# Hybrid FoX/RWKV-7 block on one core: odd chunks in the other PSUM half, q and k stored once per pair, some work reordered or moved between engines

## The chip, the core and the metric

The kernel runs on one core of a Trainium2 chip. That core has a matrix engine (TensorE, PE in the tables; its weight loads are listed apart as PEld), three other compute engines (VectorE = DVE, ScalarE = ACT, GpSimd = POOL), and SyncE (SP), which issues most DMA transfers. Each engine works through its own queue in order. Data live in device memory, in SBUF (128 partitions) and in PSUM, where matmul results land. The metric is the device time in microseconds (us) of one execution; smaller is better.

## The reference

One transformer block on a sequence of 1024 tokens, width 1024, all in float32. Two token mixers run side by side on the same normalised input `u`, and a convolutional feed-forward network follows.

```python
proj = u @ w_in                        # q,k,v,f | r,k,v,lora inputs | two gates
# FoX attention, 8 heads of 64: causal softmax with a forget term
logits = q @ k.T * 64 ** -0.5 + cum[:, None] - cum[None, :]     # cum = cumsum(log_sigmoid(f + b))
o_fox = softmax(causal(logits)) @ v
# RWKV-7, 8 heads of 64: a state of 64 x 64 per head, one step per token
def step(state, r_t, w_t, k_t, v_t, a_t, b_t):
    sa = state @ a_t
    state = state * w_t + outer(sa, b_t) + outer(v_t, k_t)
    return state, state @ r_t
y = groupnorm(y) * ln_w + ln_b
o_rwkv = (y + sum(r * k * r_k) * v) * g                         # the second term is the bonus
merged = sigmoid(gate_fox) * (o_fox @ fox_w_out) + sigmoid(gate_rwkv) * (o_rwkv @ rwkv_w_out)
h = h + gate1 * (merged @ w_o)
h = h + gate2 * conv_ffn(modulate(rms_norm(h)))
```

## The kernel before, in words

**Stages.** Read off the trace, in us from the start of the span: to 85 the modulation and the norm; to 200 the low-rank products and the first projections; to 600 the RWKV recurrence; to 622 its tail and the first late gates; to 838 the FoX attention; to 1050 the output projections; to 1647 the feed-forward network. Large products are three products of a value split in a high and a low part (`u_hi`, `u_lo`, `hi_in`, `lo_in`).

**The recurrence.** The 1024 tokens are cut into chunks of 64. A unit is one pair of heads `p` (4) and one half `hf` of the sequence (2): 8 units of 8 chunks (`NCU`) and two heads. `pre` (L698) prepares a unit: `cum`, the running sum of decays (two scans, L715), its exponentials `el` (L719) and `en` (L721), scaled keys `bk` (L739 and L744, with a copy into the other rows on ACT at L740), the chunk products `E`, and a blockwise inversion by 31 forward-substitution steps on DVE (`t` at L784, `E` at L786) from a matrix `M` that comes back by DMA. It also fills `QA` (L811, L823) and `bon`, the bonus (L827), from the product `bs` of `head_sums` (L690). `main` (L830) then forms `uw` (L863 to L872): per chunk and head a 64x64 weight `TT` times a 64x128 operand `QA`, 16 products of two records each. Head 0 lies in partitions 0 to 63, head 1 in 64 to 127, and each head's product goes to the same half of a PSUM tile; four chunks share a tile. DVE copies one half of the columns to `Wt` (L870), ACT the other to `UV` (L872). `mz` (L875 to L885) does the same with `Wt` as weight and `E` as operand; DVE adds its results into `Zt` (L882) and `Mt` (L884). Then a chain over the chunks follows: a product `sp` on PE, and the next state `S` on ACT (L903).

**What sets the order.** PE's order is written by the program. `Weave` runs generators (`pre_chain`, `main_chain`) on a clock of its own estimates and fills the gaps with steps of large products (`ps_rkv`, `qk`, `v`, `gt`). DVE, ACT, GpSimd and SP get their order in the recurrence from a scheduler that sorts by readiness and by `add_manual_dep`, which places an instruction behind another without a wait. In the attention DVE's and ACT's order follows the program too.

**Projections that pass through memory.** `qk_steps` (L386) makes q and k; ACT evacuates the high part `qh` (L393), DVE the low part `ql` (L395), and SP stores each to `d_st`, some twice, so that one transfer loads a head. `gate_steps` (L327 to L342) makes the merge gates: Abs, Exp, Ln, a combination on DVE, Exp, and a store to `d_gate`; the last of these run when the attention has begun.

**Attention.** `load_head` (L993) lets GpSimd issue three loads per head (`stA`, `stB`, `vh`). Three chains follow: logits `lg` and softmax (`nm` L1049 row maximum, `P` L1053 exponential, L1059 normalising), transposes `tp` with a split `th`, `tl` (L1086, L1089), and products `ov` with v. `collect` (L1114) runs 32 times, 4 per head: ACT copies one half of `ov`'s rows to `o` (L1120), DVE adds the other half (L1122); after four of them GpSimd makes the split `fx` (L1129, L1130). All products go through `mm` (L141). Late products `rk_ps` fill PE's gaps.

Of the kernel before, what the change touches and what calls it, by code (L numbers as in the profile page):

```python
# [9 lines left out]
F32 = mybir.dt.float32  # L10
# [122 lines left out]
def hybrid_block(ctx: ExitStack, tc: tile.TileContext, a, out):  # L133
# [13 lines left out]
    def f32(ap):  # L147
        return ap.bitcast(F32)
# [35 lines left out]
    nw0 = cp.tile([128, 4], F32, name="nw0")  # L184
    nc.vector.tensor_scalar(nw0, V("w0", 0, 4), -1.0, None, op0=ALU.mult)
    na0 = cp.tile([128, 4], F32, name="na0")
    nc.vector.tensor_scalar(na0, V("a0", 0, 4), -1.0, None, op0=ALU.mult)
    nkk = cp.tile([128, 4], F32, name="nkk")
    nc.vector.tensor_scalar(nkk, V("k_k", 0, 4), -1.0, None, op0=ALU.mult)
    oka = cp.tile([128, 4], F32, name="oka")  # L190
# [13 lines left out]
    d_st = dr.tile([8, 4, 128, S], F32R, name="d_st")  # L204
# [39 lines left out]
    marks = {}  # L244
    late_lo = deque()
# [81 lines left out]
    def gate_steps(w, i, pps, ptag, pool, tag):  # L327
# [3 lines left out]
        for hf in range(2):  # L331
# [4 lines left out]
            g = pool.tile([128, NH], F32, tag=tag, name=f"gs{i}_{hf}")  # L336
            nc.scalar.activation(g, ps, AF.Abs)
# [3 lines left out]
            nc.scalar.activation(g, g, AF.Exp)  # L341
# [4 lines left out]
    with ExitStack() as es:  # L346
# [39 lines left out]
        def qk_steps(w, i):  # L386
            sc_ = 0.125 if i < 4 else 1.0
            for hf in range(2):
# [169 lines left out]
        with tc.tile_pool(name="lg", bufs=1, reuse_waits="tile") as lg, \  # L558
# [65 lines left out]
            def forget():  # L624
# [10 lines left out]
                for hf in range(2):  # L635
# [28 lines left out]
                    nc.sync.dma_start(f32(d_st[:, 2, 64:68, cs]), f32(r[:, 0:4, :]))  # L664
                    nc.sync.dma_start(f32(d_st[:, 3, 64:68, cs]), f32(r[:, 2:6, :]))
# [24 lines left out]
        def head_sums(ps, x, hi, lo):  # L690

            nc.scalar.copy(hi, x)
            nc.gpsimd.tensor_tensor(lo, x, f32(hi), op=ALU.subtract)
            yield 3400
            mm(ps, blk_r, hi, start=True, stop=False)
            mm(ps, blk_r, lo, start=False, stop=True)

        def pre(k, p, hf):  # L698
# [41 lines left out]
            nc.scalar.copy(bk[64:128, :, 2, :], bk[64:128, :, 0, :])  # L740
# [40 lines left out]
            for s in range(31):  # L781
                J, W = s // 4 + 1, 31 - s
                tv = t32[:, 0 : J * W].rearrange("p (j w) -> p j w", w=W)
                tt(tv, E32[:, 0:J, s : s + 1].to_broadcast([128, J, W]),  # L784
                   M32[:, s : s + 1, s + 1 : 32].to_broadcast([128, J, W]), op=ALU.mult)
# [41 lines left out]
            tt(bon, bp, vv, op=ALU.mult)  # L827
            units[p, hf] = dict(ready=ready, pcd=pcd, ar=ar, E=E, QA=QA, TT=TT, bon=bon, UV=UV)

        def main(k, p, hf):  # L830
# [32 lines left out]
            for c0 in range(0, NCU, 4):  # L863
                ps = gen(f"uw{n}{c0}")
                for c in range(c0, c0 + 4):
                    for h in range(2):
                        x = (c - c0) * 128
                        mm(ps[HS[h], x : x + 128], TT[HS[h], c, :], QA[HS[h], c, :, :], start=True, stop=True)
                pv = ps.rearrange("p (c a s) -> p c a s", a=2, s=CH)
                nc.vector.tensor_copy(Wt[:, c0 : c0 + 4, :], pv[:, :, 1, :])  # L870
                for h in range(2):
                    nc.scalar.copy(UV[HS[h], c0 : c0 + 4, h, :], pv[HS[h], :, 0, :])  # L872
# [1165 lines left out]
```

## Time and profile before

| what | us |
|---|---|
| median of three runs | 1649.11 |
| lowest and highest | 1647.68, 1651.02 |
| the profiled execution's own time | 1648.91 |
| span of its trace | 1647.1 |

The profiled execution lies 0.2 us under the median, and 1.8 us of its time lie outside the span. The mean clock that was granted to PE was 0.995 of full speed. Rows of the profile read as: start, duration, engine, line, operation, output tile, inputs, the rows by the columns of the weight, the shape of the result, and how many records the row stands for; "[2.31 <-DVE ql L395]" behind a row says how long the engine had stood before it and what ended that.

### The profile page before, as it was taken

To read this page: it belongs to the slowest core of one execution; us is meant where nothing else is said; L and a number is where in the kernel's file an instruction comes from. 1 tells how busy PE (TensorE), PEld (TensorE's weight loads), DVE (VectorE), ACT (ScalarE), POOL (GpSimd) and SP (SyncE) were. 2 spreads that over 40 slices of the span, in tenths; PEclk is the share of its full clock that TensorE was granted. 3 is DMA by queue.
4 is the path that set the end of the run, shared out by engine and by line. 5 is a ranking of instruction groups with operands and counts; after the bars stand their busy time and mean duration, and the time that the engine had idled before them with its cause. 6 is when DMAs were issued, how large, how long until landed. Compare 5 with 4: busy or idle time off the path is not lost.

```text
span 1647.1 us, 25947 instructions
## 1 busy us (share of the span) xinstructions
PE 1607.8 (98%) x9694; PEld 1339.6 (81%) x9694; DVE 1222.6 (74%) x2373; ACT 820.9 (50%) x1537; POOL 130.8 (8%) x153
## 2 busy tenths in 40 slices
PE   7999999999999999999999999999999999999998
PEld 7777788798978788888888888788888888888886
DVE  5786787878876526888679447887777777886677
ACT  5563335445445646766623235644444444555455
POOL 0011101111111010221022000000000000000000
PEclk9999999999999999999999999999999999999999
DMA  8488645543332346433197420242232232675363
GB/s 339 138 326 242 178 123 143 134 123 94 107 115 85 97 126 157 129 117 106 56 353 270 168 81 26 84 134 97 96 119 98 96 109 96 225 254 160 122 211 109
DMA packets 121645, 240.59 MB, mean 146 GB/s; under 512 B 40048, under 2 KB 48880, under 8 KB 121520
## 3 DMA queue, kind: packets, MB, share of 16 engines
q1 hardware_dynamic: 113040, 220.58, 41.0%
q0 software_dynamic: 8480, 18.37, 4.2%
q8 instruction: 76, 1.25, 0.3%
q14 instruction: 49, 0.40, 0.1%
HBM read 173.35 MB, written 65.54 MB: 145 GB/s over the span
## 4 chain that ended last, share of the span: by engine, by line
PE 58%; DVE 5%; ACT 2%; DMA 2%; issue 1%; SPq 0%; ACTq 0%; DVEq 0%
PE X L141 13%; PE D L141 13%; PE Y L141 6%; PE wo L141 5%; PE br L141 4%; PE rk_ps L141 3%; PE W L141 3%; PE gt L141 3%; PE lg L141 2%; PE ov L141 2%; PE tp L145 2%; DMA d_gate<-gs 1%; DVE nm L1049 1%; DVE P L1059 1%; DVE tl L1089 0%
## 5 line engine op out<-in xcount | busy, mean ns | idle before, releaser
L141 PE MATMUL D<-op,op 128*128 128x512 f32 x924 | 209.8, 389 | 0.0
L141 PEld LDWEIGHTS D<-op,op 128*128 128x128 f32 x924 | 173.3, 188 | 36.3 <-DVE op L1261 0.3
L141 PE MATMUL X<-T_m,S 128*128 128x512 f32 x440 | 107.8, 390 | 1.6 <-ACT T_m L1722 1.1
L141 PEld LDWEIGHTS X<-T_m,S 128*128 128x128 f32 x440 | 82.4, 188 | 20.4 <-ACT T_m L1722 2.5
L1260 ACT CAST op<-g 128x512 fp32r<-128x512 f32 x77 | 47.8, 621 | 73.8 <-PE D L141 49.0
L1261 DVE TENSOR_TENSOR op<-g,op 128x512 fp32r<-128x512 f32 x77 | 53.0, 688 | 41.4 <-ACT op L1260 41.4
L1519 DVE SCALAR_TENSOR_TENSOR c<-ab,vec,c 128x512 f32<-128x512 f32 x88 | 65.9, 750 | 18.4 <-ACT c L1522 16.8
L784 DVE TENSOR_TENSOR t<-E,M 128x60 f32<-128x60 f32 (+24 forms) x248 | 55.6, 224 | 27.9 <-DMA M<-sm 21.8
L1485 DVE TENSOR_TENSOR A<-ur,A 128x512 fp32r<-128x512 f32 x64 | 44.0, 688 | 38.7 <-ACT A L1481 38.5
L1485 DVE TENSOR_TENSOR S<-ur,S 128x512 fp32r<-128x512 f32 x66 | 45.5, 691 | 35.2 <-ACT S L1481 35.1
L274 DVE TENSOR_TENSOR lo_in<-raw_in,hi_in 128x512 fp32r<-128x512 f32 x84 | 56.7, 712 | 17.6 <-PE gt L141 4.8
L1481 ACT CAST S<-ur 128x512 fp32r<-128x512 f32 x66 | 41.0, 622 | 55.8 <-DVE ur L1474 30.6
L141 PE MATMUL Y<-T_h,S 128*128 128x512 f32 x264 | 63.6, 390 | 0.4 <-ACT T_h L1740 0.4
L141 PE MATMUL Y<-T_h,A 128*128 128x512 f32 x264 | 63.7, 389 | 0.3 <-ACT T_h L1722 0.3
L1053 ACT ACTIVATE P<-lg,nm 128x896 f32<-128x896 f32 (+3 forms) x64 | 47.4, 743 | 30.7 <-DVE nm L1049 22.5
L1481 ACT CAST A<-ur 128x512 fp32r<-128x512 f32 x64 | 39.6, 622 | 43.1 <-PE X L141 31.3
L786 DVE TENSOR_TENSOR E<-E,t 128x60 f32<-128x60 f32 (+24 forms) x248 | 56.2, 227 | 6.4
L141 PE MATMUL W<-B_f,A 128*128 128x512 f32 x252 | 60.6, 389 | 0.0
L141 PE MATMUL X<-B_b,A 128*128 128x512 f32 x252 | 60.5, 389 | 0.0
L141 PEld LDWEIGHTS Y<-T_h,S 128*128 128x128 f32 x264 | 49.5, 188 | 11.1 <-ACT T_h L1740 0.8
L141 PEld LDWEIGHTS Y<-T_h,A 128*128 128x128 f32 x264 | 49.5, 188 | 10.9 <-ACT T_h L1722 0.7
L272 ACT CAST hi_in<-raw_in 128x1024 fp32r<-128x1024 f32 x42 | 43.8, 1048 | 26.3 <-PE ps_rkv L141 11.3
(483 smaller groups left out, 4134.4 us busy)
## 6 DMA issues: line engine op xcount, KB each, us to landing
raw_in<-in_w_in SPq DMA_DIRECT2D x50, 512.0 KB, 4.0
wm<-in_w_mod SPq DMA_DIRECT2D x48, 512.0 KB, 7.3
ur<-in_w_up SPq DMA_DIRECT2D x44, 512.0 KB, 3.8
g<-d_g SPq DMA_DIRECT2D x35, 512.0 KB, 4.0
d_g<-gs SPq DMA_DIRECT2D x44, 256.0 KB, 2.0
d_g<-c SPq DMA_DIRECT2D x33, 256.0 KB, 4.4
d_st<-qh SPq DMA_DIRECT2D x64, 128.0 KB, 2.5
stA<-d_st POOLq DMA_DIRECT2D x8, 1024.0 KB, 6.9
```

The costliest lines, as they stand in the source:

```text
L141: nc.tensor.matmul(o, lhsT, rhs, start=start, stop=stop, skip_group_check=more)
L145: nc.tensor.transpose(o, i, eye)
L272: nc.scalar.copy(hi, raw)
L274: nc.vector.tensor_tensor(lo[:, c : c + NH], raw[:, c : c + NH], f32(hi[:, c : c + NH]), op=ALU.subtract)
L784: tt(tv, E32[:, 0:J, s : s + 1].to_broadcast([128, J, W]), M32[:, s : s + 1, s + 1 : 32].to_broadcast([128, J, W]), op=ALU.mult)
L786: tt(E32[:, 0:J, s + 1 : 32], E32[:, 0:J, s + 1 : 32], tv, op=ALU.add)
L1053: nc.scalar.activation(e[:, 0:n], lg[:, 0:n], AF.Exp, bias=nm[:, 0:1], accum_out=nm[:, 1:2])
L1260: nc.scalar.copy(hi, src)
L1261: tt(lo, src, f32(hi), op=ALU.subtract)
L1481: nc.scalar.copy(hi, src)
L1485: tt(lo, src, f32(hi), op=ALU.subtract)
L1519: stt(c, ab[:, x + hf * NH : x + hf * NH + NH], V("conv_w", 22 * x + i), c, op0=ALU.mult, op1=ALU.add)
```

## The change

The edits, in the order of the diff:

- Four small constants share a tile `quads`, which also holds the softmax's `nm` columns; the `nm` tiles go.
- q and k are stored once per pair of heads into `d_qk` (hi and lo of each; two stores of 128 partitions for each half instead of six of 64), and the forget rows into `d_f`. A head is loaded by five transfers instead of three.
- The decay scans of the next unit stand behind the bonus product of the unit ahead (`behind(i, "bonus")`). In the first unit the copy into `QA` and the bonus stand ahead of the first substitution step (`after_this`). The last Exp of a gate and the high copy for the bonus stand behind the next `S` of a running state chain (`behind_state`, `state_done`).
- The copy inside `bk` is done by GpSimd instead of ACT.
- `uw` and `mz`: even chunks go to tile 0 as before, odd chunks to tile 1 with the two heads in exchanged halves of PSUM. Their evacuation reads tile 0 at once for `Wt` and `Zt`, and tile 1 by halves: three DVE instructions for two. `UV` and `Mt` keep four each.
- Gates that run in the attention take their buffer from the attention's pool (`Ps`), each behind the gate ahead of it.
- `collect` for heads 0 to 6: ACT copies both halves (the second into `o2`, one buffer), and GpSimd adds them. Head 7 stays with DVE.

```diff
-    nw0 = cp.tile([128, 4], F32, name="nw0")
+    quads = cp.tile([128, 32], F32, name="quads")
+    nw0, na0, nkk, oka = (quads[:, 4 * x : 4 * x + 4] for x in range(4))
...
-    d_st = dr.tile([8, 4, 128, S], F32R, name="d_st")
+    d_qk = dr.tile([4, 4, 128, S], F32R, name="d_qk")
+    d_f = dr.tile([8, 2, 4, S], F32R, name="d_f")
...
+    first_step = []
+
+    def after_this(i):
+        for x in first_step:
+            tc.add_manual_dep(x.ins, i.ins.name, NOSYNC)
+
+    held = []
+
+    def behind(i, x):
+        if x in marks:
+            tc.add_manual_dep(i.ins, marks[x].ins.name, NOSYNC)
+
+    def behind_state(i):
+        if marks.get("chain"):
+            held.append(i)
+        else:
+            behind(i, "S")
+
+    def state_done(i, last):
+        marks["S"], marks["chain"] = i, not last
+        for x in held:
+            behind(x, "S")
+        held.clear()
+
...
-            g = pool.tile([128, NH], F32, tag=tag, name=f"gs{i}_{hf}")
-            nc.scalar.activation(g, ps, AF.Abs)
+            g = marks["spare"].tile([128, NH], F32, tag="Ps", name=f"gs{i}_{hf}", bufs=2) if "spare" in marks else \
+                pool.tile([128, NH], F32, tag=tag, name=f"gs{i}_{hf}")
+            i0 = nc.scalar.activation(g, ps, AF.Abs)
+            if "spare" in marks and "gate_end" in marks:
+                tc.add_manual_dep(i0.ins, marks["gate_end"].ins.name, NOSYNC)
...
-            nc.scalar.activation(g, g, AF.Exp)
+            marks["gate_end"] = nc.scalar.activation(g, g, AF.Exp)
+            behind_state(marks["gate_end"])
...
-                h0 = 2 * (i % 4)
-                for t, k, r0 in ((hi, 0, 0), (lo, 0, 64), (hi, 2, 0)) if i < 4 else ((hi, 1, 0), (hi, 1, 64), (lo, 3, 0)):
-                    for h in range(2):
-                        nc.sync.dma_start(f32(d_st[h0 + h, k, r0 : r0 + 64, cs]), f32(t[h * 64 : h * 64 + 64, :]))
+                for t, x in ((hi, 0), (lo, 1)) if i < 4 else ((hi, 2), (lo, 3)):
+                    nc.sync.dma_start(f32(d_qk[i % 4, x, :, cs]), f32(t))
...
-        def head_sums(ps, x, hi, lo):
+        def head_sums(ps, x, hi, lo, behind_it=False):
...
-            nc.scalar.copy(hi, x)
+            i = nc.scalar.copy(hi, x)
+            if behind_it:
+                behind_state(i)
...
-                nc.vector.tensor_tensor_scan(cum[:, c0 : c0 + 256], cst2[:, 128:384], cum[:, c0 : c0 + 256], initial=0.0,
-                                             op0=ALU.mult, op1=ALU.add)
+                i = nc.vector.tensor_tensor_scan(cum[:, c0 : c0 + 256], cst2[:, 128:384], cum[:, c0 : c0 + 256], initial=0.0,
+                                                 op0=ALU.mult, op1=ALU.add)
+                behind(i, "bonus")
...
-            nc.scalar.copy(bk[64:128, :, 2, :], bk[64:128, :, 0, :])
+            nc.gpsimd.tensor_copy(bk[64:128, :, 2, :], bk[64:128, :, 0, :])
...
-                tt(tv, E32[:, 0:J, s : s + 1].to_broadcast([128, J, W]),
-                   M32[:, s : s + 1, s + 1 : 32].to_broadcast([128, J, W]), op=ALU.mult)
+                i = tt(tv, E32[:, 0:J, s : s + 1].to_broadcast([128, J, W]),
+                       M32[:, s : s + 1, s + 1 : 32].to_broadcast([128, J, W]), op=ALU.mult)
+                if k == 0 and s == 0:
+                    first_step.append(i)
...
-            nc.vector.tensor_copy(QA[:, :, 0, :], c3(q))
+            after_this(nc.vector.tensor_copy(QA[:, :, 0, :], c3(q)))
...
-            yield from head_sums(bp, rkb, tmp("kr", dt=F32R), tmp("al", dt=F32R))
+            yield from head_sums(bp, rkb, tmp("kr", dt=F32R), tmp("al", dt=F32R), True)
...
-            tt(bon, bp, vv, op=ALU.mult)
+            marks["bonus"] = tt(bon, bp, vv, op=ALU.mult)
+            after_this(marks["bonus"])
+            first_step.clear()
...
-            for c0 in range(0, NCU, 4):
-                ps = gen(f"uw{n}{c0}")
-                for c in range(c0, c0 + 4):
-                    for h in range(2):
-                        x = (c - c0) * 128
-                        mm(ps[HS[h], x : x + 128], TT[HS[h], c, :], QA[HS[h], c, :, :], start=True, stop=True)
-                pv = ps.rearrange("p (c a s) -> p c a s", a=2, s=CH)
-                nc.vector.tensor_copy(Wt[:, c0 : c0 + 4, :], pv[:, :, 1, :])
+            ps = [gen(f"uw{n}{e}") for e in range(2)]
+            for c in range(NCU):
+                for h in range(2):
+                    x = c // 2 * 128
+                    mm(ps[c % 2][HS[h ^ c % 2], x : x + 128], TT[HS[h], c, :], QA[HS[h], c, :, :], start=True, stop=True)
+            pv = [x.rearrange("p (c a s) -> p c a s", a=2, s=CH) for x in ps]
+            nc.vector.tensor_copy(Wt[:, 0::2, :], pv[0][:, :, 1, :])
+            for h in range(2):
+                nc.vector.tensor_copy(Wt[HS[h], 1::2, :], pv[1][HS[1 - h], :, 1, :])
+            for e in range(2):
...
-                    nc.scalar.copy(UV[HS[h], c0 : c0 + 4, h, :], pv[HS[h], :, 0, :])
+                    nc.scalar.copy(UV[HS[h], e::2, h, :], pv[e][HS[h ^ e], :, 0, :])
...
-            for c0 in range(0, NCU, 4):
-                ps = gen(f"mz{n}{c0}")
-                for c in range(c0, c0 + 4):
-                    for h in range(2):
-                        x = (c - c0) * 128
-                        mm(ps[HS[h], x : x + 128], Wt[HS[h], c, :], E[HS[h], c, h, 1:3, :], start=True, stop=True)
-                pv = ps.rearrange("p (c a s) -> p c a s", a=2, s=CH)
-                tt(Zt[:, c0 : c0 + 4, :], pv[:, :, 0, :], ar[:, 1, c0 : c0 + 4, :], op=ALU.add)
+            ps = [gen(f"mz{n}{e}") for e in range(2)]
+            for c in range(NCU):
+                for h in range(2):
+                    x = c // 2 * 128
+                    mm(ps[c % 2][HS[h ^ c % 2], x : x + 128], Wt[HS[h], c, :], E[HS[h], c, h, 1:3, :], start=True, stop=True)
+            pv = [x.rearrange("p (c a s) -> p c a s", a=2, s=CH) for x in ps]
+            tt(Zt[:, 0::2, :], pv[0][:, :, 0, :], ar[:, 1, 0::2, :], op=ALU.add)
+            for h in range(2):
+                tt(Zt[HS[h], 1::2, :], pv[1][HS[1 - h], :, 0, :], ar[HS[h], 1, 1::2, :], op=ALU.add)
+            for e in range(2):
...
-                    tt(Mt[HS[h], c0 : c0 + 4, HS[h]], pv[HS[h], :, 1, :],
+                    tt(Mt[HS[h], e::2, HS[h]], pv[e][HS[h ^ e], :, 1, :],
...
-                marks["S"] = nc.scalar.activation(S[-1], sp[:, c, :], AF.Copy, scale=pcd[:, c : c + 1])
+                state_done(nc.scalar.activation(S[-1], sp[:, c, :], AF.Copy, scale=pcd[:, c : c + 1]), c == last_c)
...
+        rows = d_qk[h // 2, :, h % 2 * 64 : h % 2 * 64 + 64, :].rearrange("k r s -> r k s")
...
-        nc.gpsimd.dma_start(A, d_st[h, 0:2, :, :].rearrange("k r s -> r k s"))
+        nc.gpsimd.dma_start(A[0:64, :, :], rows[:, 0:3:2, :])
+        nc.gpsimd.dma_start(A[64:128, :, :], rows[:, 1:3, :])
...
-        nc.gpsimd.dma_start(B[0:68, :, :], d_st[h, 2:4, 0:68, :].rearrange("k r s -> r k s"))
+        nc.gpsimd.dma_start(B[0:64, :, :], rows[:, 0:4:3, :])
+        nc.gpsimd.dma_start(B[64:68, :, :], d_f[h].rearrange("k r s -> r k s"))
...
-            nm = at.tile([128, 3], F32, tag="nm", name=f"nm{h}_{i}", bufs=4)
+            nms.append(nms.popleft())
+            nm = nms[0]
...
-            yield weave.use("ACT", weave.now, 270) + 140 - weave.now
-            tt(o[rows, oc], o[rows, oc], ov_ps[64 - h % 2 * 64 : 128 - h % 2 * 64, :], op=ALU.add)
-            t = weave.use("DVE", weave.now, 340) + 140
-            ov_free.append(t + 70)
+            others = ov_ps[64 - h % 2 * 64 : 128 - h % 2 * 64, :]
+            if h < 7:
+                o2 = at.tile([128, 256], F32, tag="o2", name=f"o2_{h}_{I}", bufs=1)
+                nc.scalar.copy(o2[rows, :], others)
+                yield weave.use("ACT", weave.now, 560) + 140 - weave.now
+                ov_free.append(weave.now + 70)
+                nc.gpsimd.tensor_tensor(o[rows, oc], o[rows, oc], o2[rows, :], op=ALU.add)
+            else:
+                yield weave.use("ACT", weave.now, 270) + 140 - weave.now
+                tt(o[rows, oc], o[rows, oc], others, op=ALU.add)
+                t = weave.use("DVE", weave.now, 340) + 140
+                ov_free.append(t + 70)
```

PE's queue at `uw` of the first unit (`ps_rkv` is a large product for a later unit; x8 counts products). Before:

```order
L141 MATMUL ps_rkv_2259<-u_hi,hi_in_2112 128x512 x8
L141 MATMUL uw_00_2269<-QA_0_1426,TT_0_1572 64x128 x8
L141 MATMUL uw_04_2281<-QA_0_1426,TT_0_1572 64x128 x8
L141 MATMUL ps_rkv_2259<-u_lo,hi_in_2112 128x512 x8
L141 MATMUL ps_rkv_2259<-u_hi,lo_in_2113 128x512 x6
L141 MATMUL mz_00_2308<-E_0_1425,Wt_0_2268 64x128 x8
```

After, the same stretch (the two rows of `uw` stand there four times):

```order
L141 MATMUL ps_rkv_2209<-u_hi,hi_in_2070 128x512 x8
L141 MATMUL uw_00_2219<-QA_0_1404,TT_0_1546 64x128 x2
L141 MATMUL uw_01_2220<-QA_0_1404,TT_0_1546 64x128 x2
...
L141 MATMUL ps_rkv_2209<-u_lo,hi_in_2070 128x512 x8
L141 MATMUL ps_rkv_2209<-u_hi,lo_in_2071 128x512 x6
L141 MATMUL mz_00_2259<-E_0_1403,Wt_0_2218 64x128 x2
L141 MATMUL mz_01_2260<-E_0_1403,Wt_0_2218 64x128 x2
```

The two tiles now alternate chunk by chunk; the number of products and the fillers between `uw` and `mz` are the same.

DVE's queue in the first unit, where the substitution begins (`M` comes by DMA; `ql` frees the PSUM tile of `qk`). Before:

```order
L395 SCALAR_TENSOR_TENSOR ql_0_1605<-qk_0_1461,qh_0_1603 128x512
L784 TENSOR_TENSOR t_0_1504<-E_0_1502,M_0_1497 128x31
L786 TENSOR_TENSOR E_0_1502<-E_0_1502,t_0_1504 128x31
L823 COPY QA_0_1426<-q_0_1638 128x8x64
L784 TENSOR_TENSOR t_0_1504<-E_0_1502,M_0_1497 128x30
```

After:

```order
L422 SCALAR_TENSOR_TENSOR ql_0_1579<-qk_0_1435,qh_0_1577 128x512
L853 COPY QA_0_1404<-q_0_1608 128x8x64
L857 TENSOR_TENSOR bon_0_1649<-bs_0_1626,v_637 128x512
L812 TENSOR_TENSOR t_0_1478<-E_0_1476,M_0_1471 128x31
L742 SCALAR_TENSOR_TENSOR cum_1_1655<-cst_118,cum_1_1655 128x256 x2
L297 TENSOR_TENSOR lo_in_1682<-raw_in_1679,hi_in_1681 128x512
L816 TENSOR_TENSOR E_0_1476<-E_0_1476,t_0_1478 128x31
L297 TENSOR_TENSOR lo_in_1682<-raw_in_1679,hi_in_1681 128x512
L422 SCALAR_TENSOR_TENSOR ql_1_1675<-qk_1_1583,qh_1_1673 128x512
```

The next `ql` (1675 here, 1705 before) stood behind seventeen substitution instructions of this unit, the bonus and two `lo_in`; it now stands behind two of them, the bonus, the two scans and two `lo_in`.

ACT's queue at the head of the state chain of the second unit (`el` and `en` belong to the third). Before:

```order
L719 ACTIVATE el_0_3408<-cum_0_3402 128x8x64
L740 COPY bk_1_2864<-bk_1_2864 64x8x64
L272 CAST hi_in_3026<-raw_in_3024 128x1024
L721 ACTIVATE en_0_3411<-cum_0_3402 128x512
L903 ACTIVATE S_10_3010<-sp_1_2947,pcd_1_1759 128x64
```

After:

```order
L906 COPY UV_1_1803<-uw_11_2817 64x4x64 x2
L420 ACTIVATE qh_0_2849<-qk_0_2771 128x512
L295 CAST hi_in_2964<-raw_in_2962 128x1024
L939 ACTIVATE S_10_2952<-sp_1_2889,pcd_1_1725 128x64
L420 ACTIVATE qh_1_2956<-qk_1_2855 128x512
```

The exponential `en` and the copy inside `bk` no longer stand between the cast and the first `S`.

More of the change, by code (lines that the diff above doesn't have):

```diff
@@ L663, in forget @@
                     nc.scalar.activation(r[:, 5, :], f32(r[:, 1, :]), AF.Copy, scale=-1.0)
-                    nc.sync.dma_start(f32(d_st[:, 2, 64:68, cs]), f32(r[:, 0:4, :]))
-                    nc.sync.dma_start(f32(d_st[:, 3, 64:68, cs]), f32(r[:, 2:6, :]))
+                    nc.sync.dma_start(f32(d_f[:, 0, :, cs]), f32(r[:, 0:4, :]))
+                    nc.sync.dma_start(f32(d_f[:, 1, :, cs]), f32(r[:, 2:6, :]))
             for p in range(4):
@@ L988, in hybrid_block @@
     at = es.enter_context(tc.tile_pool(name="at", bufs=2, reuse_waits="tile"))
+    marks["spare"] = at
     pl = es.enter_context(tc.tile_pool(name="pl", bufs=2, space=PS))
@@ L1013, in hybrid_block @@
         probs, av_queue, halves = {}, deque(), {}
+        nms = deque(quads[:, 16 + 3 * x : 19 + 3 * x] for x in range(4))
         ov_ps = pb.tile([128, NH], F32, tag="big", name="ov")[:, 0:256]
```

3 lines of the change are left out of this document (removed).

## The prediction

> **What bounds the kernel now.** I read the page's busy table first, then busy time by stage, then what PE waited for, and last the timelines at the places of the change.
>
> ```profile
> span 1647.1 us, 25947 instructions
> PE 1607.8 (98%) x9694; PEld 1339.6 (81%) x9694; DVE 1222.6 (74%) x2373; ACT 820.9 (50%) x1537; POOL 130.8 (8%) x153
> ```
>
> ```profile
> core 0: us, PE busy (x) PEld busy (x) DVE busy (x) ACT busy (x) POOL busy (x), PEclk, DMA share, GB/s
> 200.00:600.00 400.00, 395.38 (x3874) 331.74 (x3873) 295.81 (x838) 201.23 (x387) 48.90 (x66) 1.00 0.40 113
> ...
> 622.00:838.00 216.00, 208.24 (x1250) 179.99 (x1251) 173.72 (x347) 142.87 (x322) 35.24 (x40) 0.99 0.43 129
> ```
>
> PE is busy for 98% of the span, in the recurrence (second row) for 395 of 400 us, in the attention for 208 of 216. So time is won only where PE does its own work faster, or out of the 39 us in which it stands. The waits say how much of that lies near the edits:
>
> ```profile
> engine line waited for: us in total, times, longest us
> PE rk_ps L141 <- ACT gm L1163: 3.1, 3, 1.9
> PE sp L141 <- ACT S L903: 2.8, 4, 1.4
> PE qk L141 <- DVE ql L395: 2.3, 1, 2.3
> PE ov L141 <- DVE o L1122: 2.0, 1, 2.0
> ```
>
> Some 10 us at most can come from waits; anything larger must come from the products.
>
> **uw and mz, the largest term.** From PE's timeline of the fifth unit:
>
> ```profile
> 414.23 0.27 PE L145 MATMUL at<-cst,ar 128*128 128x128 f32 x1
> 414.34 0.27 PE L145 MATMUL vt<-cst,v 128*128 128x128 f32 x1
> ...
> 419.06 0.69 PE L141 MATMUL xi<-X,E 32*32 32x32 f32 x32
> ...
> 425.57 1.96 PE L141 MATMUL uw<-QA,TT 64*64 64x128 f32 x32
> 427.46 0.98 PE L141 MATMUL v<-hi_v,u_hi 128*128 128x256 f32 x6
> ...
> 430.98 1.96 PE L141 MATMUL mz<-E,Wt 64*64 64x128 f32 x32
> 432.87 0.34 PE L141 MATMUL sp<-UV,E 128*64 128x64 f32 x4
> 433.04 0.29 PE L141 MATMUL yp<-E,UV 128*64 128x64 f32 x4
> 433.15 0.29 PE L141 MATMUL sp<-UV,E 128*64 128x64 f32 x4
> ```
>
> A record that uses the whole array and makes 128 columns starts 0.11 us after the one ahead (414.23, 414.34). The 32 records of `uw` take 427.46 - 425.57 = 1.89 us, 0.059 each: two at a time, the two heads in two quarters of the array. Two quarters stay empty. `sp` and `yp` fill both column halves of the array with different weights, and four records of 64 columns start within 0.11 us (433.04 to 433.15): 0.028 a record, 0.055 for 128 columns, so column halves run side by side. The heads of `uw` show that diagonal quarters do. Four quarters at once should therefore take 32 / 4 = 8 steps of 0.11 = 0.88 us where 16 x 0.11 = 1.76 stood, and the other 0.13 of the 1.89 stays. The rate needed, 0.027 a record, is that of `sp`, and `xi` goes faster still (32 records in less than its 0.69). Saved: 0.88 us in each of 16 stretches (8 units, `uw` and `mz`), **-14.1 us**. Bounds: nothing, if the empty quarters don't run beside the full ones, and -14.1, since four quarters are all there are. I take the full amount, as the `sp` row is the nearest.
>
> **What the new layout costs behind PE.** The evacuations:
>
> ```profile
> L872 ACT COPY UV<-uw x32: 355/367/369, 236.0 to 575.1; 64x256 f32<-64x256 f32 x32
> L870 DVE COPY Wt<-uw x16: 415/418/425, 235.5 to 573.8; 128x256 f32<-128x256 f32 x16
> ```
>
> ```profile
> L884 DVE TENSOR_TENSOR Mt<-mz,cst x32: 405/418/428, 240.6 to 580.2; 64x256 f32<-64x256 f32 x32
> L882 DVE TENSOR_TENSOR Zt<-mz,ar x16: 415/424/426, 240.2 to 579.5; 128x256 f32<-128x256 f32 x16
> ```
>
> An instruction costs 0.42 us over 64 partitions as over 128, so one more for `Wt` and one for `Zt` per unit is 16 x 0.42 = 6.7 us of DVE. DVE has 400 - 296 = 104 us free in this stage. Nor can the first half now be read while the second is made: reading starts when all is done and takes 3 x 0.42 = 1.25 us for `Wt` and 4 x 0.37 = 1.5 for `UV`. The cover is the large product between `uw` and `mz`, 430.98 - 427.46 = 3.5 us, and PE's list of waits has no entry at `mz`. If that cover is gone because DVE comes late, two reads that used to overlap cost 0.84 each time, 13.4 us. I take +1.0, near the lower end (0 to +13.4), because 3.5 is over twice 1.5.
>
> **The first unit.** DVE, then PE, then the stretch as a whole:
>
> ```profile
> 182.54 0.19 DVE L784 TENSOR_TENSOR t<-E,M 128x31 f32<-128x31 f32 x1 [6.66 <-DMA M<-sm]
> ...
> 186.43 0.68 DVE L827 TENSOR_TENSOR bon<-bs,v 128x512 f32<-128x512 f32 x1
> ...
> 188.49 0.68 DVE L395 SCALAR_TENSOR_TENSOR ql<-qk,qh 128x512 fp32r<-128x512 f32 x1
> ```
>
> ```profile
> 182.65 1.98 PE L141 MATMUL qk<-u_lo,hi_in 128*128 128x512 f32 x8
> ...
> 189.22 3.61 PE L141 MATMUL qk<-u_hi,hi_in 128*128 128x512 f32 x8 [2.31 <-DVE ql L395]
> ```
>
> ```profile
> 186.50:193.00 6.50, 4.20 (x12) 2.99 (x11) 6.09 (x22) 1.04 (x2) 0.00 (x0) 0.74 0.58 136
> ```
>
> DVE stands 6.66 us for `M`, then runs the substitution with `ql` queued behind; PE stands 2.31 for that `ql`, and after the stop eight products take 3.61 instead of 1.98, at a granted clock of 0.74. Now `QA` and the bonus use the time in which DVE stands, and `ql` follows the first step by two scans over 256 columns (each under the 0.68 of a 512-column row), two `lo_in` of about 0.68 and a 0.19: 182.54 + 0.19 + 1.36 + 1.36 + 0.19 = 185.6, done by 186.3, where PE asks for it at 189.22 - 2.31 = 186.9. Stop and slow clock go: 2.31 + 1.63 = **-3.9** (0 if a `lo_in` stands for its cast or `M` comes later). The 64 fewer stores of q and k leave SP's queue ahead of the transfers that fetch `M`, so it isn't later for that reason. No engine waits for the scans until `el`, and PE has filler then.
>
> **The state chain.** ACT at the second unit's first `S`:
>
> ```profile
> 296.47 0.63 ACT L721 ACTIVATE en<-cum 128x512 f32<-128x512 f32 x1 [0.21 <-DVE bk L744]
> 297.01 0.29 ACT L903 ACTIVATE S<-sp,pcd 128x64 f32<-128x64 f32 x1
> ```
>
> An `S` takes 0.29, what stands ahead of it 0.63 (the `bk` copy is of that size too). With `en`, bonus copy, gate Exp and `bk` copy out of the way, PE's 2.8 us for `S` go: **-2.8** (0 to -2.8; the next to be late is a cast of 1.05 that stays ahead). What is put behind `S` is late by an `S` or two, and its users, the bonus sum and a gate store, come 3 us and more later. The `bk` copy on GpSimd stands behind one memory fill and holds `E`'s products, which `Weave` puts 10 us later: nothing.
>
> **Late gates at the stage's end.**
>
> ```profile
> ACT gs L337 <- DMA d_gate<-gs: 4.6, 1, 4.6
> ```
>
> ACT waits 4.6 us for a store to free the gate's buffer, and PE's 1.9 at `rk_ps` lies behind it. Another pool's buffers take away that store, but the new order behind the last Exp puts a new wait there: **-1.0**, between 0 and -3.1, nearer to 0 as `gm` may be late by itself.
>
> **Attention.** DVE's adds, GpSimd's queue, and the two engines side by side:
>
> ```profile
> L1120 ACT COPY o<-ov x32: 353/367/369, 645.5 to 820.4; 64x256 f32<-64x256 f32 x32
> L1122 DVE TENSOR_TENSOR o<-o,ov x32: 416/420/424, 648.2 to 820.8; 64x256 f32<-64x256 f32 x32
> ```
>
> ```profile
> POOL stA L995 <- PE lg L141: 48.8, 5, 16.7
> ...
> POOL vh L999 <- PE ov L141: 30.9, 6, 11.7
> ...
> POOL hi_in L266 <- PE rk_ps L141: 15.3, 3, 11.5
> ```
>
> ```profile
> 724.52 0.75 DVE L1059 TENSOR_SCALAR P<-P,nm 128x1024 f32<-128x1024 f32 x1
> ...
> 725.77 1.81 DVE L1059 TENSOR_SCALAR P<-P,nm 128x256 f32<-128x256 f32 x1
> ```
>
> ```profile
> 726.13 1.29 POOL L1130 TENSOR_TENSOR fx<-o,fx 128x512 fp32r<-128x512 f32 x1
> ```
>
> 28 adds leave DVE (28 x 0.42 = 11.8 us of its 174 of 216) and 28 copies of 0.37 join ACT (10.3, of 143). `ov` is then free after two copies, 0.74, instead of a copy, a handover and an add, and the 2.0 us that PE stood for `o` goes. Against it: a GpSimd add of 256 columns is about half of 1.29, 0.65, and such an instruction can hold DVE. The normalising of 256 columns took 1.81 us and ended as GpSimd did (727.58 against 727.42), where 1024 columns took 0.75. So 28 x 0.65 = 18.1 us of holding is the worst end, and -7.8, PE's whole idle time here (216.0 - 208.24), the best. With 42 us of DVE free I put the holds at +1.0, so **-1.0** in all. The five loads per head, two more than before, lie a whole head ahead of their use.
>
> The Trainium skill ("GPSIMD Engine Reference", Specifications) says that GpSimd shares its SBUF interfaces with VectorE, with contention where VectorE runs a two-port mode or has two SBUF inputs; by that rule every normalising step that meets an add is held, and the term would be +17 instead of -1. The 1.81 us row agrees that holds occur.
>
> **Sum.** -14.1 + 1.0 - 3.9 - 2.8 - 1.0 - 1.0 = -21.8 against the profiled execution's own 1648.9: **1627 us**. That execution lies 0.2 under the median, so it is the same against that. With the terms' ends near their middles this case holds from 1617 to 1637.
>
> **The rivals.**
> *B, the quarters don't run side by side.* Odd and even chunks of a head read the same array rows; if only different row halves overlap, two stay at a time and the 14.1 are not won: 1641. `sp` speaks against it. The Trainium skill ("TensorE: Matmul & The Clock Gate", Part 3, The mechanism) says that weight loads overlap running matmuls only where the row group differs, which gives this result; the rate of the `sp` rows, which hold all rows, does not agree.
> *D, DVE gives it back.* The quarters work, but `Wt` comes late each time, +13.4 - 1.0: 1639. For it: DVE's order here is the scheduler's. Against: 3.5 us of cover.
> *C, slower: ACT stands at the second copy.* `o2` has one buffer, so each copy waits for the GpSimd add ahead of it, and that add stands in one queue with loads and casts that wait for PE, 48.8 + 30.9 + 15.3 = 95 us in all. ACT then holds exponentials and `th`, and PE. It decides from 1652.4 - 1627 = 25.4 of the 95. If a third reaches PE, 32 us: 1659. For it: waits up to 16.7 us. Against: they end at a head's last logits, ahead of most of its collects.
> *E, the parts cancel*: D with holds near the middle, about 1648.
>
> **Chances.** A measurement of this kernel tells about 0.2%, 3.3 us, from no change. Forecast 0.60, B 0.12, D 0.09, C 0.14, E 0.05. Faster: 0.60 + 0.12 + 0.09 = 0.81, same 0.05, slower 0.14. The range 1616 to 1645 leaves out C and E.
>
> **What would show it.** Right: `uw` and `mz` near 1.0 us a stretch, no 2.31 at `qk`, no `S` and no `o` in PE's waits. Wrong: stretches still of 1.89 (B), waits at `mz` for `Wt` or at `sp` for `Mt` (D), ACT idle at the second copy until a GpSimd add (C), or more rows of the normalising near 1.8 us.

## The result, and the profile after

The changed kernel takes 1656.95 us (median; 1653.16 to 1659.86), the kernel before 1648.57 on the same chips: a ratio of 1.0045, with a 95% interval of 1.0035 to 1.0056. That is 8 us slower. The forecast was 1627 us, 22 us faster, with 1645 as the upper end.

The profiled execution (1657.33 us) by its page, and busy time by stage:

```profile
span 1655.6 us, 25937 instructions
PE 1602.7 (97%) x9694; PEld 1330.6 (80%) x9694; DVE 1223.6 (74%) x2361; ACT 828.1 (50%) x1557; POOL 165.7 (10%) x205
```

```profile
core 0: us, PE busy (x) PEld busy (x) DVE busy (x) ACT busy (x) POOL busy (x), PEclk, DMA share, GB/s
200.00:600.00 400.00, 380.25 (x3786) 314.33 (x3785) 304.94 (x863) 193.68 (x374) 53.82 (x71) 0.98 0.36 105
...
622.00:838.00 216.00, 206.49 (x1250) 178.45 (x1249) 162.89 (x312) 153.12 (x346) 62.26 (x84) 1.00 0.52 125
```

PE has less to do, yet the span is 8.5 us longer: in the recurrence PE stood 4.6 of 400 us before and stands 19.8 now, and its clock fell to 0.98. From the first `xi` to the last `yp` it takes 7.3 us more (table below): PE stands 11.2 us more, the busy time of uw and mz falls by 11.0, and the granted clock is low in three stretches, which costs up to 0.50 x 6.8 + 0.26 x 6 + 0.28 x 6, some 6.6 us:

```profile
227.10:233.90 6.80, 5.89 (x43) 4.75 (x44) 4.49 (x20) 1.77 (x3) 0.00 (x0) 0.50 0.18 69
...
470.00:476.00 6.00, 4.61 (x42) 3.19 (x43) 2.64 (x12) 3.23 (x6) 1.27 (x1) 0.74 0.42 128
518.00:524.00 6.00, 3.93 (x20) 2.72 (x20) 2.96 (x5) 2.55 (x4) 3.17 (x3) 0.72 0.53 175
```

PE's waits in the whole span:

```profile
PE xi L141 <- DVE X L874: 4.4, 2, 4.0
PE ov L141 <- DVE tl L1131: 3.6, 5, 1.1
PE v L141 <- DVE vs L991: 3.6, 2, 2.3
...
PE va L141 <- POOL Wts L720: 3.0, 2, 2.1
...
PE mu L141 <- POOL Wtr L720: 2.1, 3, 0.9
...
PE sp L141 <- ACT S L939: 1.1, 1, 1.1
```

The waits for `ql` at `qk`, and most of those for `S`, are gone. In their place stand new ones, most of them for DVE, and 5.1 us for GpSimd (at `va` and `mu`). The uw product of the fifth unit:

```profile
430.07 1.10 PE L141 MATMUL uw<-QA,TT 64*64 64x128 f32 x32
431.10 0.98 PE L141 MATMUL v<-hi_v,u_hi 128*128 128x256 f32 x6
```

It takes 1.03 us instead of 1.89: the four quarters run side by side as forecast (1.01), and so in all eight units; `mz` runs at that pace in four of the eight. So most of the gain on the products was made, and the time was lost around them.

### The profile page after: what moved, and what is told of

The parts are those of the page before. It is cut to its first block, busy times and chain, and to the rows that moved or that the text cites. A ratio compares the mean times of both kernels' runs of the same rounds, so it can differ in the third digit from the quotient of the medians.

```text
span 1655.6 us, 25937 instructions
## 1 busy us (share of the span) xinstructions
PE 1602.7 (97%) x9694; PEld 1330.6 (80%) x9694; DVE 1223.6 (74%) x2361; ACT 828.1 (50%) x1557; POOL 165.7 (10%) x205
## 4 chain that ended last, share of the span: by engine, by line
PE 62%; DVE 12%; DMA 3%; ACT 2%; issue 2%; SPq 1%; POOL 1%; DVEq 0%; ACTq 0%; POOLq 0%
PE X L141 14%; PE D L141 13%; PE Y L141 7%; PE wo L141 5%; PE br L141 5%; PE rk_ps L141 4%; PE gt L141 3%; PE W L141 3%; PE ov L141 2%; PE lg L141 2%; DVE E L816 2%; DVE t L812 1%; PE tp L145 1%; DMA M<-sm 1%; DVE quads L1091 1%
## 5 line engine op out<-in xcount | busy, mean ns | idle before, releaser
L1569 DVE SCALAR_TENSOR_TENSOR c<-ab,vec,c 128x512 f32<-128x512 f32 x88 | 65.9, 750 | 18.4 <-ACT c L1572 16.8
L812 DVE TENSOR_TENSOR t<-E,M 128x60 f32<-128x60 f32 (+24 forms) x248 | 56.2, 227 | 19.6 <-DMA M<-sm 13.4
L141 PE MATMUL Y<-T_h,S 128*128 128x512 f32 x264 | 63.5, 390 | 0.4 <-ACT T_h L1790 0.4
L1131 DVE TENSOR_TENSOR tl<-tp,th 128x512 fp32r<-128x512 f32 (+1 forms) x80 | 49.9, 631 | 15.2 <-ACT th L1128 15.0
```

The costliest lines, as they stand in the source:

```text
L141: nc.tensor.matmul(o, lhsT, rhs, start=start, stop=stop, skip_group_check=more)
L812: i = tt(tv, E32[:, 0:J, s : s + 1].to_broadcast([128, J, W]), M32[:, s : s + 1, s + 1 : 32].to_broadcast([128, J, W]), op=ALU.mult)
L1131: tt(tl[:, 0:w], tp[:, 0:w], f32(th[:, 0:w]), op=ALU.subtract)
L1569: stt(c, ab[:, x + hf * NH : x + hf * NH + NH], V("conv_w", 22 * x + i), c, op0=ALU.mult, op1=ALU.add)
```

## The experiments

Intervals are of the ratio to the kernel before; its median was 1648.5 to 1649.4 in these comparisons. The two right columns are from the traces: from the start of the first unit's `xi` to the end of the last `yp`, and the part of it in which no record runs on PE. A trace is one execution, in this table up to 3.5 us off its kernel's median (`first_free` 3.5 below, `first_scans` 3.4 above). The three `half` kernels leave out every second substitution step, so they don't compute the block; they tell about time alone.

| kernel | us | ratio, 95% | xi to yp | PE empty |
|---|---|---|---|---|
| before | 1648.6 | | 370.3 | 4.6 |
| changed | 1656.95 | 1.0035 to 1.0056 | 377.6 | 15.8 |
| no_quarters | 1656.31 | 1.0025 to 1.0049 | 376.8 | 6.5 |
| dve_adds | 1655.69 | 1.0022 to 1.0049 | 376.4 | 15.7 |
| scans_free | 1649.31 | 0.9981 to 1.0004 | 374.9 | 18.4 |
| first_free | 1651.59 | 1.0003 to 1.0028 | 369.5 | 12.2 |
| scans_only | 1648.43 | 0.9984 to 1.0001 | 372.0 | 5.5 |
| first_scans | 1654.78 | 1.0020 to 1.0042 | 377.9 | 7.0 |
| quarters_only | 1646.36 | 0.9968 to 0.9991 | 370.7 | 13.9 |
| quarters_wt_act | 1644.48 | 0.9960 to 0.9981 | 364.9 | 10.2 |
| half_before | 1647.86 | 0.9986 to 1.0010 | 368.0 | 2.8 |
| half_quarters | 1643.42 | 0.9953 to 0.9978 | 365.4 | 8.6 |
| half_wt_act | 1637.94 | 0.9925 to 0.9953 | 360.9 | 7.4 |

### Which part loses, which part wins

The first theory after the result (S): the scans behind the bonus crowd DVE during the substitution. Rivals: the new evacuations (Q), or GpSimd's adds (G).

`quarters_only` is the kernel before with the new uw and mz:

```diff
-                        mm(ps[HS[h], x : x + 128], TT[HS[h], c, :], QA[HS[h], c, :, :], start=True, stop=True)
+                    mm(ps[c % 2][HS[h ^ c % 2], x : x + 128], TT[HS[h], c, :], QA[HS[h], c, :, :], start=True, stop=True)
...
```

> The kernel before with only the new placement of uw and mz and its evacuations; scans, stores, states and collects are as before. Theory S (the decay scans, now behind the bonus, stretch the substitution on DVE; the four quarters pay as forecast): the stretches of uw and mz take 1.1 us instead of 1.97, nothing else moves, 1636 us (1634 to 1641). Rival Q (the evacuations that start only after the last product, and the third read, make DVE late and give the gain back): 1647 us or more, with PE waiting for Wt at mz.

`scans_free` is the changed kernel without one line, `no_quarters` and `dve_adds` the changed kernel with the old uw and mz, and with the old collect:

```diff
-                behind(i, "bonus")
```

> The changed kernel without the rule that puts the decay scans behind the bonus product of the unit ahead; everything else of the change stays. Theory S: the scans go back to the time in which DVE stands, the 31 substitution steps of the first unit take some 33 us instead of 37.9, PE's wait of 4.0 us at xi and most others of the recurrence go, 1640 us (1634 to 1646). Rival Q: the waits come from the evacuations, so 1654 us or more.

> The changed kernel with uw and mz, and their evacuations, as before; the rest of the change stays. Theory S: the 14 us that the quarters save are lost, though part of them is hidden where PE waits for DVE in any case: 1662 us (1659 to 1671). Rival Q: the evacuations were the harm, 1650 us or less.

> The changed kernel with the attention's outputs collected as before (one ACT copy, one DVE add); the rest of the change stays. Theory S, by which the loss lies in the recurrence: 1657 us (1654 to 1660). Rival G (GpSimd's adds hold DVE's normalising and ACT's second copy waits for GpSimd): 1651 us or less.

Measured: 1646.36, 1649.31, 1656.31 and 1655.69. The scan rule costs 7.6 us in the changed kernel (1656.95 - 1649.31). GpSimd's adds cost nothing that is clear of the noise. `dve_adds` is where theory S had it. The other three lie between the theories: `scans_free` is over S's 1646 and under Q's 1654, and the quarters win 2.7 us alone, where theory S had 13, and nothing clear within the changed kernel, since taking them out gives 1656.31. So there are two questions: what the scan rule does, and where the quarters' gain goes.

### The scan rule needs a partner

```diff
# scans_only: before, with
+                behind(i, "bonus")
# first_free: changed, without
-            after_this(marks["bonus"])
# first_scans: before, with both rules
+                behind(i, "bonus")
+            after_this(marks["bonus"])
```

(`first_free` and `first_scans` leave out, or add, the same rule at the copy into `QA`.)

> The kernel before with only the rule that puts the decay scans behind the bonus of the unit ahead. Theory S: the rule by itself stretches the substitution and makes xi wait, 5 to 9 us slower than before, 1654 to 1658, with PE's wait at xi or later in the recurrence. Rival I (the rule hurts only together with the other edits): 1647 to 1651.

> The changed kernel without the rule that puts QA and the bonus ahead of the first substitution step; the scan rule and the rest stay. Theory F (the scan rule hurts because the bonus of the first unit was moved ahead, which brings the next unit's scans and scaling into the first substitution): 1650 us (1648 to 1652), without the 4.0 us wait at xi. Rival K (the scan rule's partner is another edit): 1655 or more.

> The kernel before with the two DVE rules alone: scans behind the bonus, and QA and bonus ahead of the first substitution step. Theory F: the pair by itself costs what the scan rule costs in the changed kernel, 1654 us or more. Rival K: 1646 to 1650, as with the scan rule alone (1648.4).

The scan rule alone is harmless (1648.43), so theory S in its first form fell. Without its partner the changed kernel drops to 1651.59, and the pair alone makes the kernel before slower, 1654.78 against 1649.4. The partner alone was not run on the kernel before; in the changed kernel without the scan rule it stands at 1649.31. The trace of the changed kernel shows part of how; first DVE where the first unit's substitution begins and ends, then PE:

```profile
180.87 0.69 DVE L857 TENSOR_TENSOR bon<-bs,v 128x512 f32<-128x512 f32 x1 [3.60 <-PE bs L141]
181.48 0.18 DVE L812 TENSOR_TENSOR t<-E,M 128x31 f32<-128x31 f32 x1
181.58 1.27 DVE L742 TENSOR_TENSOR_SCAN cum<-cst,cum 128x256 f32<-128x256 f32 x2
...
217.37 0.68 DVE L742 TENSOR_TENSOR_SCAN cum<-cst,cum 128x256 f32<-128x256 f32 x1
217.97 1.27 DVE L297 TENSOR_TENSOR lo_in<-raw_in,hi_in 128x512 fp32r<-128x512 f32 x2
219.15 0.20 DVE L816 TENSOR_TENSOR E<-E,t 128x8 f32<-128x8 f32 x1
...
227.05 0.43 DVE L874 STREAM_TRANSPOSE X<-TT 32x256 f32<-32x256 f32 x1 [3.38 <-DMA TT<-se]
```

```profile
227.62 0.28 PE L141 MATMUL xi<-X,E 32*32 32x32 f32 x2 [3.99 <-DVE X L874]
...
229.28 2.93 PE L141 MATMUL qk<-u_lo,hi_in 128*128 128x512 f32 x6
```

```profile
228.00:234.00 6.00, 5.71 (x41) 4.68 (x42) 3.73 (x18) 1.77 (x3) 0.00 (x0) 0.51 0.05 17
```

Before, the substitution ran from 182.5 to 215.6, 33.1 us, and `X` began at 221.6, 5.4 us ahead of `xi`:

```profile
215.11 0.50 DVE L786 TENSOR_TENSOR E<-E,t 128x8 f32<-128x8 f32 x1
...
221.62 0.43 DVE L842 STREAM_TRANSPOSE X<-TT 32x256 f32<-32x256 f32 x1 [0.71 <-DMA TT<-se]
```

The bonus ahead of the first step lets the next units' scans start at once, inside the substitution, which now takes 219.35 - 181.48 = 37.9 us; between its first and last step stand 40 other DVE instructions of 25.2 us in all, where 34 of 21.7 us stood. `X`, which also needs a transfer there and back, comes 5.4 us later (the substitution ends 3.7 later, the rest is the transfer's), and PE stops for 4.0 us. After the stop the granted clock is 0.51 for 6 us (2.9 us more). Together that is 6.9 us, near the 7.6 that the scan rule costs beside its partner: `scans_free` has no stop there.

The first step could also have come sooner in the changed kernel. DVE stood 3.60 us for `bs` (the `bon` row above), but SP had issued the transfers of `M` from 173.68 to 175.4, and none of the run's took more than 3.9 us to land, so `M` was there by 179.3. Without the first-unit rule (`first_free`, second row below) the steps begin 5.2 us sooner:

```profile
173.68 1.71 SPq L804 DMA_DIRECT2D M<-sm  x4
```

```profile
176.33 0.80 DVE L812 TENSOR_TENSOR t<-E,M 128x31 f32<-128x31 f32 x1 [2.42 <-DMA M<-sm]
```

`first_scans` has the same stop at `xi`, and two stretches of low clock:

```profile
PE xi L141 <- DVE X L857: 4.1, 2, 3.8
```

```profile
227.20:234.00 6.80, 6.26 (x44) 4.90 (x44) 4.15 (x20) 1.77 (x3) 0.00 (x0) 0.50 0.36 88
302.30:305.70 3.40, 3.40 (x11) 2.82 (x11) 3.37 (x6) 1.16 (x4) 1.72 (x1) 0.50 0.56 130
```

Its first `xi` starts at 227.4, though, and at 227.0 in the kernel before, which had lost 3.9 us at `qk` ahead of it. So against the kernel before the pair gave back the first unit's gain, and the loss lies behind `xi`: 7.6 us in these traces, 2.4 of them PE standing and some 5 the clock (half of 6.8 and of 3.4).

The first unit of `scans_free` is 4.2 us quicker than before (59.7 us from the first `p` to the first `xi`, 63.9 before), near the 3.9 that was forecast. Single traces scatter: 62.0 to 65.2 us in the kernels with the full substitution and neither rule, 59.7 to 61.3 with the first-unit rule alone of the two, 63.5 to 64.8 with both; with the scan rule alone there are two traces, 60.9 and 65.1.

### Where the quarters' gain goes

uw and mz together take 20.4 us of PE in the changed kernel and took 31.4, 15.7 each (busy times):

```profile
L141 PE MATMUL mz<-E,Wt 64*64 64x128 f32 x256 | 11.6, 277 | 1.8 <-DVE t L812 1.4 <-ACT E L848 0.2 <-DVE Wt L903 0.2
L141 PE MATMUL uw<-QA,TT 64*64 64x128 f32 x256 | 8.8, 275 | 0.0
```

In the kernel with the quarters alone they take 20.0, but PE stood 9.3 us more. A stretch in which they lie, 225 to 255 us, in the kernel before, with the quarters, and with the last of the next edits:

```profile
225.00:255.00 30.00, 29.70 (x292) 23.98 (x291) 28.25 (x90) 14.27 (x28) 2.02 (x4) 1.00 0.47 128
```

```profile
225.00:255.00 30.00, 27.55 (x284) 20.95 (x283) 27.91 (x91) 12.03 (x24) 2.37 (x4) 1.00 0.43 119
```

```profile
225.00:255.00 30.00, 28.47 (x291) 22.56 (x290) 18.61 (x45) 14.36 (x29) 2.86 (x5) 1.00 0.51 130
```

DVE is busy for 28.25 of 30 us there: the substitution of the next unit runs while PE makes uw and mz. Other units are alike before the change, except the last two (22.96 of 25 us from 375 to 400, for one). What DVE owes to PE is not ready sooner because PE asks sooner. In the kernel with the quarters alone PE waits most for the state in the recurrence, 6.4 us where it waited 2.8, and then for DVE directly. Below are the two largest waits, one late product, and (last) what delayed one state, on ACT:

```profile
PE sp L141 <- ACT S L907: 6.4, 6, 2.4
...
PE v L141 <- DVE vs L959: 2.1, 2, 1.8
```

```profile
237.05 2.12 PE L141 MATMUL mz<-E,Wt 64*64 64x128 f32 x32 [0.27 <-DVE Wt L869]
```

```profile
249.29 0.61 ACT L740 COPY bk<-bk 64x512 f32<-64x512 f32 x1 [1.75 <-DVE bk L739]
249.94 0.32 ACT L907 ACTIVATE S<-sp,pcd 128x64 f32<-128x64 f32 x1
```

mz takes 2.12 instead of 1.10 as the later of DVE's reads of uw are missing, and `S` stands behind a copy that waited for DVE. To test DVE's pace, its load was changed:

```diff
# half_before, half_quarters, half_wt_act
-            for s in range(31):
+            for s in range(0, 31, 2):
# quarters_wt_act, half_wt_act, told, best: Wt by ACT
-            nc.vector.tensor_copy(Wt[:, 0::2, :], pv[0][:, :, 1, :])
+            nc.scalar.copy(Wt[:, 0::2, :], pv[0][:, :, 1, :])
# told: PE's planner, after uw and after mz
+            weave.now -= 860
```

> The kernel before with every second of the 31 substitution steps left out (some 7 us of DVE less per unit, where it stands beside uw, mz and the state chain). It is the base of the next run. Theory D (DVE's full stretches set the pace of the recurrence): a few us faster than before, 1640 to 1646, since little waiting of PE is left to win there. Rival P (PE alone sets the pace): 1648, as before.

> The same shortened substitution with the quarters of uw and mz. Theory D: with DVE relieved the quarters pay what they save on PE, at least 9 us under the run with the shortened substitution alone (14 at most). Rival R (the saving is lost elsewhere, to ACT, transfers or the order of PE): 4 us or less under it, as without the shortening (2.7).

> The kernel before with the quarters, and the three copies to Wt done by ACT, in front of the UV copies of the same tile, in place of DVE. ACT stood 5.8 us ahead of the first UV copy. Theory D: Wt is there 1.5 us after uw, DVE has 10 us less to do in the full stretches, and part of what the quarters save shows: 1640 us (1636 to 1643). Rival R: 1645 to 1648, as with DVE's copies.

> The kernel before with the quarters and ACT's copies to Wt, and PE's planner told that uw and mz are 0.86 us shorter each (its clock is set back by that), so that it places filler products by the true time. Theory W (the rest of the quarters' saving is lost because PE's written order still counts 1.97 us and reaches DVE's and ACT's results early): 1638 us (1635 to 1642). Rival V (the results of DVE and ACT set the pace whatever PE's order): 1643 to 1646, as without.

> The shortened substitution (every second of the 31 steps left out), the quarters, and ACT's copies to Wt. Theory D2 (DVE's pace takes the quarters' saving: with half of the substitution gone and Wt off DVE, most of the saving shows): 1639 us or less, 9 us under the shortened substitution alone (1647.9). Rival R2 (another part of the loop from unit to unit, the state chain on ACT and DVE's last evacuations, keeps it): 1641 to 1644, as with DVE's copies.

Half of the substitution left out wins nothing by itself (1647.86): PE was full. With the quarters it gives 4.4 us, less than the 9 that theory D asked for; ACT's copies give 1.9 over the quarters with DVE's copies. That 1.9 isn't clear of the noise, as the intervals overlap. Both together give 9.9 us (1647.86 to 1637.94), of the 12.5 by which the busy time of uw and mz falls there (31.4 to 18.9). So DVE's side holds the gain: with one remedy 4.4 or 4.7 us of it show, against the same kernel without the quarters or against before, with both most of it. What isn't separated: fewer steps also shorten each unit's way to `X`, not only DVE's load, and ACT's copies were not run without the quarters. PE's order as far as tested isn't the reason: with the planner told the true length it took 1646.03 (0.9963 to 0.9985), no better than 1644.48.

### Smaller edits

```diff
# scans_free_bk_act: scans_free, with
-            nc.gpsimd.tensor_copy(bk[64:128, :, 2, :], bk[64:128, :, 0, :])
+            nc.scalar.copy(bk[64:128, :, 2, :], bk[64:128, :, 0, :])
# scans_state_free: scans_free, without
-            behind_state(marks["gate_end"])
...
-                behind_state(i)
# qk_only: before, with
+                    nc.sync.dma_start(f32(d_qk[i % 4, x, :, cs]), f32(t))
...
# scans_free_old_qk: scans_free, with the storage of before
+    d_st = dr.tile([8, 4, 128, S], F32R, name="d_st")
...
```

> The changed kernel without the rule for the decay scans, and with the copy inside bk on ACT again. Theory H (GpSimd's copy holds DVE, or DVE's neighbours hold it, in the full stretches): 1646 us or less, 3 us under the run without the rule alone. Rival T (the copy is off the path): 1649, no difference.

> The changed kernel without the scan rule and without the rule that puts the gates' last Exp and the bonus copy behind the next S. Theory O (that rule makes what stands behind it late and costs the 3 us by which the run without the scan rule is over the quarters alone): 1646 us or less. Rival N (the rule is neutral): 1649, as without the scan rule alone.

> The kernel before with only the storage of q and k once per pair (32 stores of 256 KB for 96 of 128, five loads per head for three). Prediction's step: nothing, 1649 (1647 to 1651). Rival L (two more loads per head on GpSimd's queue delay its sums and the heads): 1652 or more, from the recurrence's last units and the first logits.

> The changed kernel without the scan rule and with the old storage of q and k. Theory L (the storage costs 3 us, as it did by itself): 1646 us (1645 to 1648). Rival: the 3 us of the storage alone don't add, 1649.

The `bk` copy (1649.27) and the rule behind `S` (1649.73) change nothing against 1649.31. The copy isn't always out of the way, though: in the last unit of the changed kernel it took GpSimd 3.18 us (0.8 in most units, 0.62 on ACT before), `Wts` stood behind it, and PE stood 2.1 us for `Wts`, in the stretch with the clock of 0.72:

```profile
515.16 3.18 POOL L768 COPY bk<-bk 64x512 f32<-64x512 f32 x1 [6.33 <-DVE bk L767]
518.42 1.60 POOL L720 TENSOR_TENSOR Wts<-ysq,Zts 128x512 fp32r<-128x512 f32 x1
```

Whether this costs time beside the scan rule was not run. The storage of q and k costs 3 us alone: 1652.48 (1.0008 to 1.0026), against the prediction's nothing. But with the old storage `scans_free` takes 1653.42 (1.0015 to 1.0038), 4 us more, so its cost does not add, and what decides it stays open.

### A better version

The kernel before with the quarters and ACT's copies (`quarters_wt_act`) is the fastest that computes everything, 0.9971 (0.9960 to 0.9981), though not clear of `quarters_only` and `told`. The first unit's order added to it, scans free (the run `best`):

> The kernel before with the quarters, Wt copied by ACT, and the first unit's order alone (QA and bonus ahead of the first substitution step, scans free). Theory S: the first unit's gain of some 4 us adds to that of the quarters with ACT's copies (4.7): 1640 us (1638 to 1643). Rival I (the first unit's gain is taken back by a later wait): 1644 or more.

It took 1646.50 (0.9975 to 0.9995), no gain, so rival I held. The first `xi` came 61.2 us after the first `p` (65.2 without the rule), but the rest of the recurrence took 370.2 (364.9): PE was early and waited, 2.0 us at `xi` and up to 3.8 at an `S`.

## Why the prediction was wrong

- **uw and mz, -14.1**: the products ran side by side as forecast (1.03 us a stretch, 1.01 expected; half of the `mz` took longer), so rival B fell, and with it the rule of the Trainium skill ("TensorE: Matmul & The Clock Gate", Part 3, The mechanism) as far as it says that weight loads overlap only across row groups: odd and even chunks of a head share one, and ran together. The step that failed is the sentence on cover, "DVE has 400 - 296 = 104 us free in this stage" and +1.0 for the evacuations. That is an average; where uw and mz lie DVE was busy 28.25 of 30 us. The cover of 3.5 us was that of `mz` alone, and PE waits for other results of DVE too. The term measured about -2.7 alone, and nothing clear in the changed kernel. This is rival D's place, and what is lost, 11 to 14 us, is near its 13.4. That is luck in part: D had late `Wt` at `mz` or late `Mt`, and with the quarters alone PE's list has 0.3 us for `Wt` (2.4 more lie inside `mz`, busy for 11.2 where uw is for 8.8) and 6.4 for the state `S`, which on ACT stood behind work that had waited for DVE. The Trainium skill ("TensorEngine Tiling (Array Packing)", PSUM Bottleneck) warns that PSUM evacuation may become the bottleneck after such tiling and advises ScalarE and VectorE both; ACT's `Wt` copies agree in sign, but their 1.9 us are within the noise.
- **First unit, -3.9**: right for the part costed (`ql` no longer stops PE at `qk`), and 4.2 us show in the trace of `scans_free`, though the run `best` gave them back later. Wrong was "No engine waits for the scans until `el`": the scans and what follows them were put into the substitution, `X` came late, and PE stood 4.0 us at `xi` where it had stood 2.31 at `qk`. Nor did DVE still have the time standing for `M` that the bonus was to use: it stood 3.60 us for `bs` instead. The scan rule cost nothing alone and 7.6 us beside its partner, and the pair 5.4 in the kernel before; the prediction costed each by itself, and no rival had it.
- **State chain, -2.8**: PE's wait for `S` fell from 2.8 to 1.1 us, but without the rule behind `S` the time was the same (1649.73 against 1649.31, both without the scan rule), so 0. The `bk` copy, put at nothing as GpSimd was thought to have only `E`'s products behind it, held `Wts` once and PE with it.
- **Late gates, -1.0**: from the last `yp` to the first `lg` 29.6 us instead of 31.1, -1.5; the kernel with the quarters alone, with its old buffers, has 28.8, so the edit isn't shown to be the cause.
- **Attention, -1.0**: 0. From the first `lg` to the first `br` it took 192.0 us before and after. The wait for `o` went, that for `tl` rose from 1.7 to 3.6. Holding by GpSimd occurred: the 64 normalising steps took 36.1 us in all before and now

```profile
L1101 DVE TENSOR_SCALAR P<-P,quads 128x896 f32<-128x896 f32 (+3 forms) x64 | 40.5, 633 | 2.3
```

  4.4 us more, where rule and bound gave up to 18 (the term at that bound is -1.0 - 1.0 + 18.1, some +16, not +17); with the old collect (`dve_adds`) they take 36.1 again. Rival C didn't come: putting the old collect back gave 1655.69.
- **q and k, nothing**: 3 us alone, and of the other sign beside the scans' old order.

## What to carry to other kernels

Before a shorter product is counted as won, look at the engine that feeds it in that very stretch, in a window of a few tens of us: if it is full there, PE will only wait. A rule that orders one instruction pulls along what hangs on it; check together with the other rules what enters the serial chain. A stop can cost nearly as much again by the clock that follows it, so read the granted clock behind each stop; here it fell behind some stops of 2 us and not behind others.

## What the runs showed that was not expected

After a stop of 4.0 us PE ran at a granted clock of 0.51 for the 6 us from 228 to 234. The length of a stop alone doesn't say whether the clock falls. In the kernel before, a stop of 2.31 us at `qk` was followed by 0.51 (first row); in the changed kernel a stop of 2.3 us for `vs`, from 444.3 to 446.6, by none (second row):

```profile
189.50:192.90 3.40, 3.40 (x9) 2.65 (x9) 3.02 (x13) 0.35 (x1) 0.00 (x0) 0.51 0.65 145
```

```profile
444.00:454.00 10.00, 7.69 (x72) 7.34 (x70) 9.48 (x32) 4.03 (x9) 0.77 (x1) 1.00 0.28 80
```

What decides it stays open. And a rule of order that alone left the time where it was cost 7.6 us beside another, while two remedies that each freed about a third of the quarters' gain freed about four fifths of it together.
